# Walking both halves of a gated linear recurrence through their levels together, in a one-core encoder block

## The chip, the cores and the metric

The kernel runs on one core of one Trainium2 chip. A core has five engines that run their own instruction queues: TensorE (PE, matrix products), VectorE (DVE), ScalarE (ACT), GpSimd (POOL) and SyncE (SP, which only starts transfers here). Transfers between the chip's main memory and the core's on-chip memory go through DMA queues. The metric is the device time of one execution in microseconds; lower is better. Three executions of the kernel before took 2413.86, 2413.97 and 2415.13 us (median 2413.97 us).

## What is computed

The reference is one layer of a streaming-encoder block on 256 tokens of width 2048, all in 32-bit floats:

```python
x = x + 0.5 * swiglu(rms_norm(x, ffn1_norm[l]), ffn1_w_up[l], ffn1_w_down[l])
h = rms_norm(x, mix_norm[l])
proj = h @ w_in[l]
q_a, f_a, i_a, g_a, x_b, gate_b, gates = jnp.split(proj, splits, axis=-1)
o_a = hgrn2_chunked(q_a..., f_a..., i_a..., lb)        # gated linear recurrence, 8 heads
y_a = rms_norm(o_a, hgrn_norm[l]) * silu(g_a)
y_b = rglru_branch(x_b, gate_b, ...)                   # conv(4), then an associative scan
merged = g[:, :, 0] * (y_a @ w_branch_a[l]) + g[:, :, 1] * (y_b @ w_branch_b[l])
x = x + merged @ w_out[l]
x = x + cross_attention(rms_norm(x, xattn_norm[l]), rms_norm(mem, mem_norm[l]), ...)
x = x + 0.5 * swiglu(rms_norm(x, ffn2_norm[l]), ffn2_w_up[l], ffn2_w_down[l])
return rms_norm(x, final_norm)
```

The part that the change touches most is the gated linear recurrence. For each of 8 heads the state is S_t = diag(f_t) S_{t-1} + (1 - f_t) outer v_t and the output o_t = S_t^T q_t; it is not computed token by token.

## The kernel before, in words

**Weights.** Nearly all the time goes to products of the 256 tokens with weight tiles of 128 x 2048 numbers. Each weight comes in by one transfer into a tile `raw`; ACT copies it, rounded, into `h`, and DVE subtracts to get the rest, `l`. PE multiplies with both, which keeps the precision of 32-bit floats. `raw`, `h`, `l` and a few others share a ring of nine large buffers called `big`. Between the two SwiGLU parts there are 160 such weights: 48 for the input projection (`win`, `wv`), 32 gate weights (`wg`), then the branch, output, query, key and output weights of the rest. On PE a weight of the input projection is a row of 16 matmuls with `h` and one of 16 with `l` (`acc<-ops,h`, `acc<-ops,l`); a value or gate weight has 16 and 8 (`acc<-h,ops`, `acc<-l,ops`).

**The recurrence.** `hgrn(hf)` (from line 1264) is a Python generator that writes down the work for half the heads, four of them: `q`, `f` and `k` for 128 features x 4 heads x 256 tokens. It goes through seven levels (1, 2, 4, ... 64 tokens). At each level PE makes small products of `k` with `q` (`acc<-silu,k`: blocks of 32 partitions up to level 32, then 64 and 128), DVE masks them into the tile `S`, and DVE multiplies one half of `q` and one of `k` by the running products `tots`. Behind the levels come the outputs (`acc<-S,v`, two banks for two heads), their squares on ACT (`osq`), a sum over features on PE (`acc<-osq,ones`), a root on ACT (`ostd`), and on DVE two `RECIPROCAL`s and four products into `ya`. This is done twice, for two heads each. Each `yield` is a point at which the main loop goes on with another weight. `lru(hf)` (line 1366), the other recurrence, has the same form.

The main loop walks a list of units; behind each unit it takes steps of the first generator in the list `side`:

```python
    units += [lambda hf=hf: side.append(hgrn(hf)) or True]      # behind each half's 16 weights

    for u in units:
        if not u():
            pump(2)
```

So the first half's levels are written between the second half's input weights, and the second half's levels behind those.

**Sums made ahead.** The second SwiGLU part needs for 56 of its up-projection tiles four differences of quarter tiles each. They are made during the 160 weights in the middle: `make_sums` loads a tile (`made<-wu`, started by POOL), DVE does four subtractions of 128 x 512 (`made<-made`), and POOL starts the store (`kept<-made`). `make_ahead` spreads the 56 over a number of weights that `between` and a constant set.

**What sets the order.** Nothing runs in the order in which it was written. Every operation is recorded (`Flow.record`), and a planner (`arrange`) gives each a price and a due time, and plays the engines forward: each takes the ready operation with the earliest due time, as far as a free buffer is there. The sequence that comes out is the program; each engine then runs its part of it strictly in that order. Buffers are given out in the same pass, the eight banks in which PE accumulates (`psum`, tag `acc`) too. All instructions of the profile carry line 478, where the sequence is issued, so one goes by the names of the tiles.

The pools for the middle part are opened in one line. `scores` holds the tile `S` of a half, and `tmp2` the tiles `junk` and `ostd`:

```python
    middle.enter_context(scope(tmp=8, tmp2=2, scores=1, extra=2, feature=3))
```

## Time and profile before

| | |
|---|---|
| median of three executions | 2413.97 us |
| the profiled execution: its time, its span | 2415.09 us, 2413.3 us |
| PE busy in the span | 2401.9 us (100%) |
| DVE busy | 2088.1 us (87%) |
| ACT busy | 1441.9 us (60%) |
| granted TensorE clock | 0.999 |
| first and last load for a sum made ahead | 849.3 and 1690.8 us |
| first and last small product of the recurrence | 884.1 and 1103.9 us |

A row of a timeline gives the start in us from the start of the span, the length in us, the engine, the operation, output<-inputs, the size, and in how many instructions; what stands in brackets is the idle time before it and what ended it. PE shows a 32-bit product as two passes, so 32 products of `k` with `q` read as x64. PE's instructions overlap: the step from the start of one to the start of the next tells what each costs, not its length. The same holds on DVE to a lesser degree.

### The profile page before, as it was taken

How to read it: one execution, taken by the hardware profiler on the slowest of the kernel's cores; microseconds unless marked ns; L12 is line 12 of the kernel's file. 1: busy time of each engine (PE TensorE's matmuls, PEld its weight loads, DVE VectorE, ACT ScalarE, POOL GpSimd, SP SyncE). 2: the span in 40 equal slices, each digit the busy share in tenths (PEclk: the TensorE clock that was granted, in tenths of full speed). 3: DMA queues.
4: the chain of work that ended last, by engine and by line, in shares of the span. 5: the costliest groups of instructions: out<-in, count | busy, mean ns of one | idle time of the engine just before them, and what ended most of it. 6: DMA issues, size and time to landing. Idle time of an engine off the chain costs nothing. (4 is left out here: it accounts for less than half of the span.)

```text
span 2413.3 us, 31006 instructions
## 1 busy us (share of the span) xinstructions
PE 2401.9 (100%) x12105; PEld 2005.3 (83%) x12105; DVE 2088.1 (87%) x2270; ACT 1441.9 (60%) x1432; POOL 88.3 (4%) x149
## 2 busy tenths in 40 slices
PE   9999999999999999999999999999999999999998
PEld 8888788888888888888888888888888788888887
DVE  7899999999996578888787878887799999999995
ACT  8765666766665444445853455555676666666663
POOL 0000000000000000000000000000000000000000
PEclk9999999999999999999999999999999999999999
DMA  9675877787884578798898898887798677777773
GB/s 367 242 277 181 262 261 250 257 259 255 254 258 177 190 293 317 273 347 331 332 336 334 322 367 341 333 311 274 271 378 325 244 261 262 261 262 261 262 272 116
DMA packets 101235, 674.37 MB, mean 279 GB/s; under 512 B 11232, under 2 KB 12000, under 8 KB 27232
## 3 DMA queue, kind: packets, MB, share of 16 engines
q1 hardware_dynamic: 79776, 523.40, 58.0%
q0 software_dynamic: 20592, 147.86, 19.0%
q8 instruction: 95, 1.56, 0.3%
q10 hardware_dynamic: 720, 1.13, 0.1%
q14 instruction: 52, 0.43, 0.0%
HBM read 581.12 MB, written 62.91 MB: 267 GB/s over the span
## 5 line engine op out<-in xcount | busy, mean ns | idle before, releaser
L478 DVE TENSOR_TENSOR l<-raw,h 128x2048 fp32r<-128x2048 f32 (+2 forms) x425 | 859.2, 2025 | 170.2 <-ACT h L478 78.2
L478 ACT ACTIVATE h<-raw 128x2048 fp32r<-128x2048 f32 (+2 forms) x425 | 721.8, 1704 | 380.6 <-PE acc L478 166.4
L478 PE MATMUL acc<-h,xh 128*128 128x512 f32 x1237 | 473.6, 391 | 1.0 <-DVE x L478 0.5
L478 PE MATMUL acc<-h,xl 128*128 128x512 f32 x1237 | 472.0, 389 | 0.0
L478 ACT ACTIVATE h<-td 128x1024 fp32r<-128x1024 f32 (+1 forms) x262 | 322.8, 1241 | 228.2 <-DVE td L478 204.2
L478 DVE TENSOR_TENSOR tl<-td,h 128x1024 fp32r<-128x1024 f32 (+1 forms) x262 | 374.8, 1445 | 5.1 <-PE acc L478 2.1
L478 PE MATMUL acc<-h,hidop 128*128 128x512 f32 x1408 | 355.8, 390 | 0.0
L478 PE MATMUL acc<-h,ops 128*128 128x512 f32 x1408 | 336.8, 391 | 0.0
L478 PEld LDWEIGHTS acc<-h,hidop 128*128 128x128 f32 x1408 | 262.8, 188 | 53.9
L478 PEld LDWEIGHTS acc<-h,ops 128*128 128x128 f32 x1408 | 262.7, 188 | 53.9
L478 PE MATMUL acc<-ops,h 128*128 128x512 f32 x1152 | 282.0, 393 | 0.2 <-DVE ops L478 0.2
L478 PEld LDWEIGHTS acc<-h,xh 128*128 128x128 f32 x1237 | 231.8, 188 | 53.8 <-ACT h L478 3.1
L478 PEld LDWEIGHTS acc<-h,xl 128*128 128x128 f32 x1237 | 232.3, 188 | 47.7
L478 PEld LDWEIGHTS acc<-ops,h 128*128 128x128 f32 x1152 | 211.4, 188 | 42.3 <-DVE ops L478 0.6
L478 PE MATMUL acc<-l,hidop 128*128 128x512 f32 x704 | 193.5, 389 | 0.4 <-DVE l L478 0.4
L478 PE MATMUL acc<-tl,xh 128*128 128x512 f32 x636 | 175.4, 392 | 0.8 <-DVE tl L478 0.7
L478 PE MATMUL acc<-l,ops 128*128 128x512 f32 x704 | 174.3, 389 | 0.0
L478 PE MATMUL acc<-l,xh 128*128 128x512 f32 x601 | 167.8, 390 | 0.0
L478 DVE TENSOR_TENSOR made<-made 128x512 f32<-128x512 f32 x224 | 152.1, 687 | 8.6 <-DMA made<-wu 5.2
L478 PEld LDWEIGHTS acc<-ops,l 128*128 128x128 f32 x1152 | 150.5, 191 | 6.4
L478 PEld LDWEIGHTS acc<-l,hidop 128*128 128x128 f32 x704 | 132.1, 188 | 28.2 <-DVE l L478 0.8
L478 PEld LDWEIGHTS acc<-l,ops 128*128 128x128 f32 x704 | 132.1, 188 | 27.4
(172 smaller groups left out, 2132.4 us busy)
## 6 DMA issues: line engine op xcount, KB each, us to landing
raw<-wu SPq DMA_DIRECT2D x109, 1024.0 KB, 6.2
raw<-wd SPq DMA_DIRECT2D x72, 1024.0 KB, 6.8
made<-wu POOLq DMA_DIRECT2D x56, 1024.0 KB, 6.7
kept<-made POOLq DMA_DIRECT2D x56, 1024.0 KB, 6.8
td<-kept SPq DMA_DIRECT2D x56, 1024.0 KB, 7.2
raw<-wu SPq DMA_DIRECT2D x56, 768.0 KB, 6.0
raw<-win SPq DMA_DIRECT2D x40, 1024.0 KB, 4.9
raw<-wg SPq DMA_DIRECT2D x32, 1024.0 KB, 7.1
```

Source lines behind the costliest of these rows:

```text
L478: getattr(op.queue.real, method)(*map(real, args), **{k: real(v) for k, v in kw.items()})
```

## The change

The change takes three steps.

The two halves of the recurrence are no longer started one behind the other. A new helper, `both`, takes one step of each in turn, so that level by level first half 0 and then half 1 is written, and the pair is put into `side` once, behind the second half's 16 weights. For this there are two tiles `S`. The pool `tmp2` goes from two buffers to one.

The sums made ahead begin four weights sooner: `between` starts 8 weights ahead of the end of the first SwiGLU part's list and no longer 4. The number of weights over which they are spread stays 140 (160 less 20 before, 164 less 24 now), so they end four weights sooner too.

```diff
-    between = between - 4, len(plan) - between
+    between = between - 8, len(plan) - between + 4
     plan_ffn("ffn2", wu2, wd2)
...
     def make_ahead(i):
-        n, pieces = len(MADE), between[1] - 20
+        n, pieces = len(MADE), between[1] - 24
         if 0 <= i < pieces:
             for j in range(i * n // pieces, (i + 1) * n // pieces):
                 makers.append((i + 2, make_sums(*MADE[j])))
...
-    middle.enter_context(scope(tmp=8, tmp2=2, scores=1, extra=2, feature=3))
+    middle.enter_context(scope(tmp=8, tmp2=1, scores=2, extra=2, feature=3))
...
+    def both(parts):
+        while parts:
+            for p in list(parts):
+                try:
+                    more = next(p)
+                except StopIteration:
+                    parts.remove(p)
+            if parts:
+                yield more
+
     units = []
     for hf in range(2):
...
-        units += [lambda hf=hf: side.append(hgrn(hf)) or True]
+    units += [lambda: side.append(both([hgrn(hf) for hf in range(2)])) or True]
```

**On PE, the small products.** Before, each half has its own runs of them between the weights. Here is the end of the first half's levels, where the outputs begin (`silu` is the tile of `q`; `v_6510` and `v_6516` are the values of the two halves of the tokens):

```order
L478 MATMUL acc<-silu,k 128x128 x4
L478 MATMUL acc<-ops,h 128x512 x16
L478 MATMUL acc<-ops,l 128x256 x16
L478 MATMUL acc<-S,v_6510 128x256
L478 MATMUL acc<-S,v_6516 128x128
L478 MATMUL acc<-S,v_6510 128x256
L478 MATMUL acc<-S,v_6516 128x128
L478 MATMUL acc<-ops,h 128x512 x16
L478 MATMUL acc<-ops,l 128x256 x16
L478 MATMUL acc<-osq,ones 128x256 x2
```

The same place in the changed kernel, where it lies among the gate weights:

```order
L478 MATMUL acc<-silu,k 128x128 x8
L478 MATMUL acc<-h,ops 128x512 x16
L478 MATMUL acc<-l,ops 128x512 x8
L478 MATMUL acc<-S,v_6520 128x256
L478 MATMUL acc<-S,v_6526 128x128
...
L478 MATMUL acc<-osq,ones 128x256 x2
L478 MATMUL acc<-h,ops 128x512 x16
L478 MATMUL acc<-l,ops 128x512 x8
L478 MATMUL acc<-osq,ones 128x256 x2
```

Eight rows with `S` stand there in one run and not four (the rows left out repeat the two above them three times), and a sum over squares follows at once, in the same run. In all, the runs of 32-bit products (those with `silu,k`, `S,v`, `osq`, `xc,lw`, the transposes and a few others) are 76 on PE before and 65 after; all eleven that go lie in the recurrence, which has 24 before (18 of levels, 6 of outputs and sums) and 13 after (9 and 4).

**On DVE, behind the levels.** Before, the second half's first `RECIPROCAL`s stand between the `l` of gate weights, counted from 0, number 8 to 11:

```order
L478 TENSOR_TENSOR made<-made 128x512 x3
L478 RECIPROCAL ostd<-ostd 128x256
L478 TENSOR_TENSOR l<-raw,h 128x2048
L478 TENSOR_TENSOR made<-made 128x512
L478 TENSOR_TENSOR l<-raw,h 128x2048
L478 TENSOR_TENSOR ya<-acc,ostd 128x256
L478 RECIPROCAL ostd<-ostd 128x256
L478 SCALAR_TENSOR_TENSOR ya<-ya,vt,silu 128x256
L478 TENSOR_TENSOR l<-raw,h 128x2048
```

In the changed kernel four of the eight stand behind the `l` of gate weight 4, with no other `l` until gate weight 5's, which comes 21 instructions later:

```order
L478 TENSOR_TENSOR l<-raw,h 128x2048
L478 TENSOR_TENSOR made<-made 128x512 x3
L478 RECIPROCAL ostd<-ostd 128x256
L478 TENSOR_TENSOR made<-made 128x512
L478 TENSOR_TENSOR ya<-acc,ostd 128x256
L478 RECIPROCAL ostd<-ostd 128x256
L478 SCALAR_TENSOR_TENSOR ya<-ya,vt,silu 128x256
L478 TENSOR_TENSOR ya<-acc,ostd 128x256
L478 SCALAR_TENSOR_TENSOR ya<-ya,vt,silu 128x256
L478 SCALAR_TENSOR_TENSOR xc<-plain,vt,xc 128x255 x2
L478 RECIPROCAL ostd<-ostd 128x256
```

**On DVE, the first sums made ahead**, one piece of the difference (+ is the changed kernel), among the second group of input weights:

```order
-L478 TENSOR_TENSOR l<-raw,h 128x2048
 L478 TENSOR_TENSOR silu<-silu,sum 128x256
-L478 TENSOR_TENSOR sum<-acc,lo 128x256
-L478 TENSOR_TENSOR sum<-sum,rstd 128x256
-L478 TENSOR_TENSOR l<-raw,h 128x2048
+L478 TENSOR_TENSOR l<-raw,h 128x2048
+L478 TENSOR_TENSOR made<-made 128x512 x3
+L478 TENSOR_TENSOR sum<-acc,lo 128x256
+L478 TENSOR_TENSOR made<-made 128x512
```

Four subtractions `made` stand there now, of which the kernel before has none so early. On POOL's queue the zeroing of `S` is now two `MEMSET`s in a row, behind 12 loads of tiles for sums; before it was one behind 3 and one behind 12.

## The prediction

> **What bounds the kernel now.** I read the busy times first, then PE's waits, then PE's timeline through the recurrence, and last DVE's lead over PE there.

> ```profile
> PE 2401.9 (100%) x12105; PEld 2005.3 (83%) x12105; DVE 2088.1 (87%) x2270; ACT 1441.9 (60%) x1432; POOL 88.3 (4%) x149
> ```
> ```profile
> PE warm L478 <- DVE ones L478: 1.1, 1, 1.1
> PE acc L478 <- DVE tl L478: 0.7, 3, 0.3
> PE acc L478 <- DVE x L478: 0.5, 1, 0.5
> PE acc L478 <- DVE l L478: 0.4, 1, 0.4
> PE acc L478 <- DVE ev L478: 0.3, 1, 0.3
> PE acc L478 <- DVE ops L478: 0.2, 1, 0.2
> PE acc L478 <- ACT h L478: 0.2, 1, 0.2
> ```
> ```profile
> 840.00:980.00 140.00, 140.00 (x1153) 121.05 (x1152) 105.36 (x140) 62.79 (x69) 10.17 (x18) 1.00 0.81 294
> 980.00:1130.00 150.00, 150.00 (x1184) 128.97 (x1183) 123.36 (x159) 67.37 (x69) 12.30 (x22) 1.00 0.86 320
> 1900.00:2300.00 400.00, 399.81 (x1792) 330.40 (x1791) 392.11 (x343) 244.32 (x192) 0.00 (x0) 1.00 0.71 261
> ```

> PE is busy all through; its waits (who for whom: total, times, longest) add to 3.4 us, of which 1.1 stands at the start. In the stages (length, then busy time of PE, weight loads, DVE, ACT, POOL, then clock and DMA) the clock is full. So the kernel is as long as PE's instructions, and a change can gain only by making PE's own work shorter, plus at most 2.3 us of waits. It loses whatever makes PE wait. DVE is the engine to watch: 105 of 140 us where the first half of the recurrence runs, 123 of 150 in the second, 392 of 400 late in the second SwiGLU.

> **The small products.** The change adds and removes no matmul. It turns 24 runs of 32-bit products into 13. What does a run cost beside its products?

> ```profile
> 888.53 2.07 PE L478 MATMUL acc<-ops,l 128*128 128x256 f32 x16
> 890.54 0.74 PE L478 MATMUL acc<-silu,k 128*32 128x16 f32 x64
> 891.20 3.92 PE L478 MATMUL acc<-ops,h 128*128 128x512 f32 x16
> 894.96 2.08 PE L478 MATMUL acc<-ops,l 128*128 128x256 f32 x16
> 896.87 3.82 PE L478 MATMUL acc<-ops,h 128*128 128x512 f32 x16
> 900.53 2.07 PE L478 MATMUL acc<-ops,l 128*128 128x256 f32 x16
> ...
> 974.36 1.05 PE L478 MATMUL acc<-silu,k 128*128 128x128 f32 x8
> 975.17 3.92 PE L478 MATMUL acc<-ops,h 128*128 128x512 f32 x16
> 978.93 2.08 PE L478 MATMUL acc<-ops,l 128*128 128x256 f32 x16
> 980.84 1.47 PE L478 MATMUL acc<-S,v 128*128 128x256 f32 x8
> 982.07 3.23 PE L478 MATMUL acc<-ops,h 128*128 128x512 f32 x13
> ```
> ```profile
> L478 PE MATMUL acc<-silu,k x880: 182/183/276, 884.1 to 1103.9; 128*32 128x16 f32 x128, 128*32 128x32 f32 x40, 128*64 128x64 f32 x6, 128*128 128x128 f32 x2
> ```

> Without a run between, `l` to the next `h` is 896.87 - 894.96 = 1.91 us and `h` to `l` 900.53 - 896.87 = 3.66. With one they are 891.20 - 888.53 = 2.67 and 894.96 - 891.20 = 3.76. The run costs 0.76 + 0.10 = 0.86 us. Its 64 passes start over 0.74 - 0.18 us (a pass lasts 183 ns, the middle number of the last row), so 8.9 ns apart: 0.57 us for 64. The other 0.29 us is paid per run, for going into small blocks and out again. Two runs in one pay it once, seven times (levels 1 to 32 and the diagonal): 7 x 0.29 = 2.03 us. For full-width passes only the slower first matmuls behind the run are sure, 978.93 - 975.17 - 3.66 = 0.10 us. I take 0.10 for the last level, 0.20 for 64-wide blocks, and 2 x 0.15 for the two runs of outputs and sums that go. Sum: 2.6 us less, between 11 x 0.10 = 1.1 and 11 x 0.29 = 3.2.

> [...]

> **What else is on PE's path: DVE's work, now bunched.** Both halves' level work now falls between the same input weights:

> ```profile
> L478 DVE TENSOR_TENSOR made<-made 128x512 f32<-128x512 f32 x224 | 152.1, 687 | 8.6 <-DMA made<-wu 5.2
> L478 DVE RECIPROCAL ostd<-ostd 128x256 f32<-128x256 f32 x8 | 13.9, 1744 | 1.1 <-ACT ostd L478 1.1
> ```

> Through the levels the total hardly moves. From the `l` of input weight 35 (of 48, from 0) to that of gate weight 4 the changed order has 136 DVE instructions, the one before 119; with each at its length less the 0.08 us by which DVE's instructions overlap (shown below) that is 89 us against 87, since before the first half's last products and more of `made` stood there. PE has 17 weights of at least 5.44 us there, 92 us, and the longer runs. The order leaves two weights, 11 us, from level to level, and a level's four products of 0.69 us (as long as `made`, which has the same 512 elements) are 2.8. I cost the levels at nothing; if that cover goes, each costs PE what DVE is late.

> It is tighter behind the levels. From the `l` of gate weight 4 to that of gate weight 13 the changed order gives DVE 84 instructions: 9 `l` of 2.20 us, 8 reciprocals of 1.66, 20 subtractions `made` of 0.60, 21 of `xc` of 0.40, 16 of `ya` of 0.34, 4 gates of 0.66 and `lru`'s four long ones, 66 us (the overlap: below, 1132.51 - 1132.18 = 0.33 us where the length is 0.42). PE needs for nine weights 9 x 5.44 = 49 us (1144.80 - 1139.36, below), and for a run of sums and one of `lru` in between about 4: 53 us. DVE loses 13 us of its lead. How much lead is there? The first `l` below is used at 1095.89, the second at 1114.48:

> ```profile
> 1083.16 2.28 DVE L478 TENSOR_TENSOR l<-raw,h 128x2048 fp32r<-128x2048 f32 x1
> 1098.33 2.28 DVE L478 TENSOR_TENSOR l<-raw,h 128x2048 fp32r<-128x2048 f32 x1
> 1116.27 1.41 DVE L478 SCALAR_TENSOR_TENSOR gate<-acc,rtok,bgate 128x512 f32<-128x512 f32 x2 [1.93 <-PE acc L478]
> 1132.18 0.42 DVE L478 TENSOR_TENSOR ya<-acc,ostd 128x256 f32<-128x256 f32 x1
> 1132.51 1.74 DVE L478 RECIPROCAL ostd<-ostd 128x256 f32<-128x256 f32 x1
> 1140.84 2.28 DVE L478 TENSOR_TENSOR l<-raw,h 128x2048 fp32r<-128x2048 f32 x1
> ```
> ```profile
> 1095.89 1.98 PE L478 MATMUL acc<-l,ops 128*128 128x512 f32 x8
> 1114.48 1.98 PE L478 MATMUL acc<-l,ops 128*128 128x512 f32 x8
> 1139.36 1.98 PE L478 MATMUL acc<-l,ops 128*128 128x512 f32 x8
> 1144.80 1.98 PE L478 MATMUL acc<-l,ops 128*128 128x512 f32 x8
> ```

> That is 10.5 and 13.9 us; and the last `l`, used at 1144.80, shows 1.7 left where the second half's reciprocals stand now. With 13.9 the lead comes down to about 1 and PE hardly waits; with 10.5 PE waits 2.5 us, and 4.4 if DVE also waits once for PE as it does before the gates here (1.93 us). I take 1.0 us, nearest the 13.9 (a lead taken just ahead of the gate weights, as it would be here); ends 0 and 4.4.

> **The sums made ahead.** The same 224 subtractions (152 us of DVE) and 112 transfers begin and end four weights, 22 us, earlier, at a time when DVE was at 75% or less. Nothing waits for them before the second SwiGLU. Zero, with DVE's free time as cover; from -0.5 us to +0.5 us from DVE's different load at the start of the second SwiGLU, whose waits for `tl` are part of the 0.7 above. The second tile `S` frees the second half's zeroing on POOL from waiting; zero, no one waits there. The one buffer for `ostd` makes ACT's next root wait for two reciprocals, and ACT's later `h` behind it; with leads of 10 us zero, else part of the 4.4.

> **The sum.** 2415.09 (the profiled execution) - 2.6 + 1.0 = 2413.5 us. The median of the three runs, 2413.97, is 1.1 below the profiled one; the same sum from it is 2412.4 us, which I predict. 0.2% (4.8 us) is about what a measurement of this kernel can tell from no change, so this is "no change", slightly on the fast side.

> **The rivals.**

> *The output banks (slower).* PE accumulates in eight banks. With both halves at their outputs, four hold results of the first two heads of each half, two a gate weight's, and the sums take more, so PE's next `S` run must wait until DVE has read a bank into `ya`. From the start of the first `S` run: two times 1.23 us of `S` (982.07 - 980.84), the last squares on ACT (0.38 each), table load and root, then reciprocal, `made` and `ya`:

> ```profile
> 1110.35 0.38 ACT L478 ACTIVATE osq<-acc 128x256 f32<-128x256 f32 x1 [4.53 <-PE acc L478]
> 1129.78 1.28 ACT L478 ACT_TABLE_LOAD   x1
> 1131.08 0.69 ACT L478 ACTIVATE ostd<-acc,few 128x512 f32<-128x512 f32 x1
> ```

> 2.46 + 0.9 + 1.28 + 0.69 + 1.74 + 0.69 + 0.42 = 8.2 us. PE comes to that run after 2.46 + 0.9 of sums + 5.44 + 0.9 = 9.7. The margin is 1.5 us. Three subtractions `made` stand on DVE ahead of that reciprocal, and they need a load:

> ```profile
> DMA to landing us min/median/max: 4.1/6.7/12.7
> DVE made L478 <- DMA made<-wu: 5.2, 4, 2.2
> ```

> A load as late as the longest (6.0 us over the median) costs PE 6.0 - 1.5 = 4.5 us: 2412.4 + 4.5 = 2416.9, slower than before from 1.6 + 1.5 = 3.1 us of lateness on. Against it: DVE waited for such loads four times in 224, 2.2 us at the most. [...]

> *The waits go too (faster).* DVE's load in the second SwiGLU falls so that the 2.3 us of waits behind the start vanish, none comes at the gates, and the saving is at its upper end: 2413.97 - 3.2 - 2.3 = 2408.5. For it: DVE ends the sums 22 us earlier. Against it: the largest waits lie in stages that the change does not touch.

> [...]

> *It does not do what it says.* Switching is paid per level and half anyway, inside the merged run: -0.4 for the rest, + 1.0: 2414.6.

> **How the numbers follow.** Forecast 0.56; banks 0.22, half of it with more than one late load and over 2418.8; waits go too 0.12, nearly all beyond 2409.1; passes at 4 ns 0.05; nothing merged 0.05. Faster by over 0.2%: 0.11. Slower: 0.11. Within: 0.78. The range leaves out the lower half of the fast case and the upper half of the banks': 2408.9 to 2418.0.

> **What would show it.** Runs `silu,k` of x128, about 0.18 + 127 x 0.0089 = 1.3 us long, in 9 places, and 13 runs in all; PE busy about 2399 us; the gap between `l` and its use down to about 1 us at gate weight 13; waits of PE for `l` or `ya` of 0 to 4 us between 1090 and 1160; the first load for a sum near 827 us, the last near 1669. It is wrong if PE waits at the `S` runs, if a level finds DVE not ready, or if the second SwiGLU, where DVE has 2% left, begins with DVE behind.

## The result, and the profile after

The changed kernel takes 2420.77 us, the median of seven runs; the kernel before, in seven runs on the same chip, 2413.97. The ratio is 1.0030, with a 95% interval from 1.0021 to 1.0040: slower by 0.3%, 6.8 us, where I had forecast 2412.4 and no change. The runs spread more than before: 2418.85 to 2425.35 us, against 2413.42 to 2415.93. The profiled execution is the fastest of them, 2418.85 us with a span of 2417.0 (before: 2413.3), so its trace holds 3.7 of the 6.8 us.

The busy times, and PE's waits (who for whom: total, times, longest) of the changed kernel:

```profile
PE 2398.5 (99%) x12105; PEld 2004.8 (83%) x12105; DVE 2088.9 (86%) x2270; ACT 1440.2 (60%) x1430; POOL 88.2 (4%) x149
```
```profile
PE acc L478 <- issue: 5.1, 2, 2.8
PE acc L478 <- DVE tl L478: 1.5, 3, 1.0
PE acc L478 <- DVE ops L478: 1.5, 2, 1.3
PE warm L478 <- DVE ones L478: 1.1, 1, 1.1
PE acc L478 <- ACT h L478: 0.7, 2, 0.5
...
```

PE's own work shrank by 3.4 us, to about the 2399 that I had forecast. Its waits grew from 3.4 to 10.4 us, and half of that is a kind that the profile before does not have: "issue", time in which the engine waited for nothing that the profile shows. The chain of waits from 970 to 1015 us has both of them, and PE's timeline shows what stands around each:

```profile
969.93 10.69 PE acc L478 x218
980.62 2.31 issue
982.93 24.26 PE acc L478 x325
1007.20 2.78 issue
1009.98 5.12 PE acc L478 x27
```
```profile
976.20 2.07 PE L478 MATMUL acc<-ops,l 128*128 128x256 f32 x16
978.20 1.30 PE L478 MATMUL acc<-silu,k 128*32 128x16 f32 x128
979.42 1.20 PE L478 MATMUL acc<-ops,h 128*128 128x512 f32 x4
982.93 2.93 PE L478 MATMUL acc<-ops,h 128*128 128x512 f32 x12 [2.31 <-issue]
...
1005.87 1.33 PE L478 MATMUL acc<-silu,k 128*32 128x16 f32 x128
1009.98 3.36 PE L478 MATMUL acc<-ops,h 128*128 128x512 f32 x14 [2.78 <-issue]
```

Each stands behind a merged run of x128. The first is inside one input weight: four of its 16 products run, then PE stands still, though the same tile `h` feeds the other twelve. No data is missing there. So what was?

**The instructions themselves.** The page's list of DMA queues has a line that I had passed over:

```profile
q8 instruction: 95, 1.56, 0.2%
```

Packets, MB, share: 95 packets of 16 KB during the kernel. PE's instructions in the trace (12,105 products, 12,105 weight loads, 149 others) are 24,359: 256.4 to a packet, or 95.15 blocks of 256. In experiment 12 PE has 2,560 more than before and the queue ten packets more, which is 256 to a packet. So I take it that PE's program comes in through the DMA engines while it runs, 256 instructions at a time. Counted from 0 in the order of their starts, the instruction at which PE stopped is 9665 the first time and 10433 the second: both are number 193 of a block of 256 (37 x 256 + 193 and 40 x 256 + 193). Here and below 193 is good to one instruction, since a weight load and the product ahead of it overlap and their order is read from their starts. The packets that end the waits begin at 980.67 and 1007.64, last 0.97 and 0.94 us, and PE goes on 1.3 and 1.4 us after each has landed.

A merged run is 128 products and 128 weight loads: a whole block, gone in 1.3 us. Theory A is that PE stops because it uses up its instructions faster than the next block comes. A block lasts PE 22 to 29 us where only big products stand; where a merged run falls in it, much less. What starts a fetch the trace doesn't show. Its beginning follows, by 1.4 to 10.4 us over all fetches of the kernels before and after, the moment at which PE is 320 instructions short of the one that will need it; so I reckon with 320 instructions of cover, an estimate from these two traces. If a run of 256 lies wholly in them, the other 64 are 32 big products, and the cover is 7.0 us of PE's time. In the changed kernel four fetches have about 7 us of it; in the kernel before, whose runs are 128 instructions, the least is 10.4. Of the four, the two that came late began 7.2 us after that moment, the other two 4.2 and 3.7. The closest that a block came to being late before was 4.0 us ahead of its use.

The rest of the span, by PE's place in the work (after less before): 1.5 us ahead by input weight 16, in code that did not change; 3.0 lost from there to gate weight 25; 1.7 at the queries (`ops`); 0.8 at `tl`; 0.3 regained between.

### The profile page after: what moved, and what is told of

It is laid out like the page before. It is cut to its first block, busy times and chain, and to the rows that moved or that the text cites. A ratio compares the mean times of both kernels' runs of the same rounds, so it can differ in the third digit from the quotient of the medians.

```text
span 2417.0 us, 31003 instructions
## 1 busy us (share of the span) xinstructions
PE 2398.5 (99%) x12105; PEld 2004.8 (83%) x12105; DVE 2088.9 (86%) x2270; ACT 1440.2 (60%) x1430; POOL 88.2 (4%) x149
## 4 chain that ended last, share of the span: by engine, by line
PE 95%; DVE 2%; DMA 2%; issue 1%; ACT 1%; SPq 0%; ACTq 0%; DVEq 0%; POOLq 0%
PE acc L478 95%; DMA raw<-wvm 1%; DMA l<-own 1%; DVE tl L478 0%; DVE td L478 0%; DVE l L478 0%; DVE ev L478 0%; DMA own<-wd 0%; ACT h L478 0%; DVE x L478 0%; SPq L478 0%; ACT ops L478 0%; ACT x L478 0%; DVE hidop L478 0%; ACT ev L478 0%
## 5 line engine op out<-in xcount | busy, mean ns | idle before, releaser
L478 DVE TENSOR_TENSOR l<-raw,h 128x2048 fp32r<-128x2048 f32 (+2 forms) x425 | 859.4, 2026 | 183.7 <-ACT h L478 90.2
L478 ACT ACTIVATE h<-raw 128x2048 fp32r<-128x2048 f32 (+2 forms) x425 | 721.4, 1703 | 355.9 <-PE acc L478 166.7
L478 PE MATMUL acc<-h,xh 128*128 128x512 f32 x1237 | 473.3, 391 | 1.2 <-ACT h L478 0.7
L478 PE MATMUL acc<-h,xl 128*128 128x512 f32 x1237 | 471.6, 389 | 0.0
L478 ACT ACTIVATE h<-td 128x1024 fp32r<-128x1024 f32 (+1 forms) x262 | 322.8, 1241 | 229.6 <-DVE td L478 198.3
L478 DVE TENSOR_TENSOR tl<-td,h 128x1024 fp32r<-128x1024 f32 (+1 forms) x262 | 374.5, 1445 | 4.9 <-PE acc L478 2.3
L478 PE MATMUL acc<-h,hidop 128*128 128x512 f32 x1408 | 355.5, 390 | 0.0
L478 PE MATMUL acc<-h,ops 128*128 128x512 f32 x1408 | 336.7, 391 | 0.0
L478 PEld LDWEIGHTS acc<-h,ops 128*128 128x128 f32 x1408 | 263.1, 188 | 53.9
L478 PEld LDWEIGHTS acc<-h,hidop 128*128 128x128 f32 x1408 | 262.9, 188 | 53.7
L478 PE MATMUL acc<-ops,h 128*128 128x512 f32 x1152 | 281.7, 393 | 6.6 <-issue 5.1
L478 PEld LDWEIGHTS acc<-h,xh 128*128 128x128 f32 x1237 | 231.7, 188 | 53.4 <-ACT h L478 3.5
L478 PEld LDWEIGHTS acc<-h,xl 128*128 128x128 f32 x1237 | 232.2, 188 | 47.8
L478 PEld LDWEIGHTS acc<-ops,h 128*128 128x128 f32 x1152 | 211.6, 188 | 49.3 <-issue 5.8
L478 PE MATMUL acc<-l,hidop 128*128 128x512 f32 x704 | 193.6, 389 | 0.0
L478 PE MATMUL acc<-tl,xh 128*128 128x512 f32 x636 | 174.6, 391 | 1.6 <-DVE tl L478 1.5
L478 PE MATMUL acc<-l,ops 128*128 128x512 f32 x704 | 173.9, 389 | 0.0
L478 PE MATMUL acc<-l,xh 128*128 128x512 f32 x601 | 167.5, 390 | 0.0
L478 DVE TENSOR_TENSOR made<-made 128x512 f32<-128x512 f32 x224 | 152.7, 687 | 12.4 <-DMA made<-wu 8.9
L478 PEld LDWEIGHTS acc<-ops,l 128*128 128x128 f32 x1152 | 150.7, 191 | 6.5
L478 PEld LDWEIGHTS acc<-l,hidop 128*128 128x128 f32 x704 | 132.1, 188 | 27.6 <-DVE l L478 0.2
L478 PEld LDWEIGHTS acc<-l,ops 128*128 128x128 f32 x704 | 132.2, 188 | 27.5
```

Source lines behind the costliest of these rows:

```text
L478: getattr(op.queue.real, method)(*map(real, args), **{k: real(v) for k, v in kw.items()})
```

## The experiments

Theory B, the first rival, was that the transfers of the sums made ahead, now 22 us earlier, starve PE. Theory C was that it is the two halves at one level: their tiles, banks, DVE and ACT. Comparisons are with runs of the kernel before in the same set (2414.96 us median in the first, 2414.59 in the second, 2415.22 in the third).

**1. The sums' shift alone**

```diff
-    between = between - 4, len(plan) - between
+    between = between - 8, len(plan) - between + 4
...
-        n, pieces = len(MADE), between[1] - 20
+        n, pieces = len(MADE), between[1] - 24
```

> Only the sums made ahead move four weights; the two halves of the recurrence stay one behind the other. Theory A (PE ran out of instructions behind the merged runs of 128 small products: the two waits of PE marked issue, 5.1 us, in the changed kernel): no wait marked issue here, runs stay at 64 products; what is left of the change is the waits of PE for ops near 1448 (1.5 us) and for tl near 1913 (0.8 more than before), so 2 to 3 us over the kernel before, about 2416.5. Theory B (the loads and stores of the sums, 22 us earlier, crowd the DMA engines and that alone starves PE): the waits marked issue are here too, 3 to 5 us, near 980 and 1010, and the time is 2418 to 2421.

2417.81 us, ratio 1.0014 (1.0005 to 1.0023): 2.9 us slower. No wait marked issue, and no block closer than 4.6 us. PE's waits, for `ops` above all, add to 5.0 against 3.4 us:

```profile
PE acc L478 <- DVE ops L478: 1.2, 3, 0.6
...
```

So theory B falls, and a term that I had at zero is 2.9 us. The waits hold 1.6 of it; where the rest went is not shown. The place in the second SwiGLU that I had named (`tl`) is not where it went: 0.7 us, as before.

**2. The levels alone** (`both`, and the tiles for `S` and `ostd`; `between` as before)

> Only the two halves go through their levels together (with the two tiles S and one for ostd); the sums made ahead stay where they were. Theory A: PE busy falls to about 2398.5 as in the changed kernel, the waits marked issue stand behind one to three of the merged runs of 128, 2 to 6 us in all, the waits for ops near 1448 and tl near 1913 are as small as before (0.2 and 0.7): 2413 to 2417. Theory B: no wait marked issue, 2.6 us of saving is left whole: 2411 to 2412.

2423.44 us, ratio 1.0035 (1.0022 to 1.0047), above the 2413 to 2417 of theory A. The waits marked issue are there without the sums' shift, at the same two instructions 9665 and 10433. And something more happens behind them: PE's clock falls. The waits begin at 982.29 and 1010.56 us and last 2.35 and 2.58. PE's waits, and windows behind each of the two (length, PE busy, granted clock, DMA share, GB/s):

```profile
PE acc L478 <- issue: 4.9, 2, 2.6
PE acc L478 <- ACT h L478: 3.1, 5, 1.4
```
```profile
985.30:988.70 3.40, 3.40 (x10) 0.51 0.67 265
988.80:992.00 3.20, 3.20 (x23) 1.00 0.82 276
1012.60:1016.00 3.40, 2.86 (x7) 0.51 0.99 383
```

For 3.4 us PE runs at half speed, so each of the two waits, of 2.35 and 2.58 us, costs 1.7 more. Small products, 1.3 us of them, stand ahead of these waits (more on those at 6), but they are not needed: the clock also fell behind a wait of 1.88 us for `x` in the first SwiGLU part of experiment 5, and behind one of 2.27 us for `h` in experiment 8, both among large products alone (the same columns, first of 5, then of 8):

```profile
434.70:438.00 3.30, 3.30 (x10) 0.50 1.02 271
```
```profile
1456.20:1459.50 3.30, 3.30 (x8) 0.50 1.01 410
```

The length of the wait alone doesn't decide it: the profiled execution of the changed kernel shows no such window although its waits are 2.31 and 2.78 us: the granted clock is 1.00 from 985 to 990 us and from 1010 to 1015. Three of its seven runs have a granted clock of 0.997 against its 0.999, and they are the three over 2424 us; that the clock fell at the same places there is inferred, not seen.

Also, the waits for `h` add to 3.1 us, 2.4 of it behind the levels, at gate weights 12 to 17 (0.2, 0.8 and 1.4 between 1150 and 1185 us). Experiment 10 takes that up. And the waits for `tl` are 1.5 us, where I had expected the 0.7 of the kernel before: with 0.7 in experiment 1, they come with the levels and not with the sums' shift.

**3. The instruction stream shifted**

```diff
     for _ in range(16):
         pe.matmul(warm[:, :P], ones, ones, start=True, stop=True)
+    for _ in range(18):
+        pe.matmul(warm[:, :8], ones, ones[:, :8], start=True, stop=True)
```

> The changed kernel with 18 more tiny products (8 columns) behind the 16 that warm PE at the start, where PE waits for its first weight: all later work is unchanged, but PE's instruction stream is 36 instructions longer ahead of the levels. Theory A: in the changed kernel both waits marked issue begin at the same place of a 16 KB block of instructions (instruction 193 of 256, counted from the trace), where a merged run of 256 instructions lies whole in the last 320 ahead of it; 36 more instructions move the runs so that 26 fewer of them lie there at the second and fourth merged run, some 2 us more time. Waits marked issue fall from 5.1 to between 0 and 1.5 us (the first merged run, then wholly inside, may now wait up to 1 us), time 2414.5 to 2417. Any theory by data, buffers, engines or DMA load alone: nothing changes, 5 us of waits marked issue at the same two products, 2419 to 2421.

2419.87 us (2417.73 to 2421.65), 1.0020 (1.0011 to 1.0029). A miss in part: an fp32 product is two passes (68 rows of `warm` at the start against 32), so 72 instructions were added and not 36, and they cost 4 us at the start: the first weight's products begin at 10.51 us, against 6.54 in the changed kernel, and the first 16 of them last 5.51 us against 4.32. With 72, again four fetches have 7.5 us of cover or less. But the waits went where the count says, not where they had been: one of 1.3 us in the page, inside other products than before, once more at instruction 193 of a block, number 39 x 256 + 193:

```profile
1000.20 1.83 PE L478 MATMUL acc<-ops,l 128*128 128x256 f32 x14
1003.32 0.40 PE L478 MATMUL acc<-ops,l 128*128 128x256 f32 x2 [1.29 <-issue]
```

Nothing of the data, the buffers or the order had changed. This speaks for A, and against every theory by data.

**4. No sums around the merged runs**

```diff
-            for j in range(i * n // pieces, (i + 1) * n // pieces):
+            active = lambda i: max(0, min(i, 34)) + max(0, i - 54)
+            for j in range(active(i) * n // (pieces - 20), active(i + 1) * n // (pieces - 20)):
```

> The changed kernel, but no sum is made ahead for 20 of the 140 weights, those around the merged runs (the other 120 take 0.93 sums each in place of 0.80). Theory A in its full form (the fetch of the next 16 KB of instructions stands in the DMA queues behind loads and stores of 1 MB): the fetch begins some 3 us sooner and the waits marked issue fall to 0 to 1 us; the denser sums elsewhere cost 0 to 3 us: 2414 to 2418. If only the count of instructions matters and not the DMA load: 5 us of waits marked issue stay, 2419 to 2422.

2431.34 us, 1.0073 (1.0060 to 1.0085). It did not make its own condition: started sums were emptied late, and the DMA share from 970 to 981 us was 1.01, against 0.91 from 970 to 983 in the changed kernel. One wait marked issue stayed (2.6 us, instruction 9665), the other went; the moved sums cost 8.6 us of waits for `h` elsewhere. It says nothing on the DMA's part.

**5. The kernel before, each small product issued twice**

```diff
                     s = slice(g * P + b, g * P + b + 32)
-                    pe.matmul(acc[b:b + 32, i * n:(i + 1) * n], kv[:, h, s], pick(qv[:, h, s]), start=True, stop=True)
+                    for _ in range(2):
+                        pe.matmul(acc[b:b + 32, i * n:(i + 1) * n], kv[:, h, s], pick(qv[:, h, s]), start=True, stop=True)
```

> The kernel before (halves one behind the other, sums where they were), but each product of the 32-wide runs is issued twice, the second over the first: runs as long as the merged ones (256 instructions), of one half only, with two weights from run to run. Theory A: waits marked issue appear here too, each beginning at instruction 193 of 256 of a 16 KB block, 1 to 3 us each, 4 to 14 us in all over the twelve runs; PE's busy time grows by 12 runs x 0.57 = 6.8 us, the time by 11 to 24 us (more where the clock falls behind a wait). Theory C (what starves PE comes from the two halves being at the same level: their tiles, banks, DVE, ACT): no wait marked issue, 6.8 us more and no more.

2428.81 us, 1.0059 (1.0041 to 1.0077), two runs. Three waits marked issue, 2.9 us in all, all at instruction 193 of a block, with one half at a time and no buffer changed; one falls inside a run of small products:

```profile
1028.80 0.34 PE L478 MATMUL acc<-silu,k 128*32 128x16 f32 x17
1029.93 1.26 PE L478 MATMUL acc<-silu,k 128*32 128x16 f32 x111 [0.79 <-issue]
```

Theory C falls. The total is below my 4 to 14 us: counted as above, six fetches had 7.5 us of cover or less, and three of them came in time, so little cover makes a wait possible and not certain.

**6. Bursts of dummy products far from the levels**

```diff
+    def burst(accs, n):
+        for _ in range(n):
+            pe.matmul(accs[0][:32, :8], ones[:, :32], ones[:, :8], start=True, stop=True)
```
(ahead of the gates' groups 4 to 7 with n = 32, 64, 96, 128; ahead of the output's groups 0 to 3 with 128, 96, 64, 32)

> The kernel before, with tiny dummy products (32 rows of the array's columns, 8 columns, overwritten by the product behind them) in eight places far from the levels: ahead of the gates' groups 4 to 7, bursts of 128, 256, 384 and 512 instructions, and ahead of the output's groups 0 to 3 of 512, 384, 256 and 128. Theory A: no wait marked issue behind 128; 0 to 3 us behind 256, as the burst lies to the 16 KB blocks; 2 to 8 us behind each of 384 and 512, beginning at instruction 193 of a block; so some 10 to 30 us of it in all, where no half of a recurrence is. If the waits come from the recurrence's data: none anywhere.

2483.8 us, and only one wait marked issue, 1.9 us. The expectation was wrong on the speed: products that all write the same group of 32 columns ran at 36 ns a pass (128 passes in 4.66 us), four times the 8.9 of the levels, whose products go round four groups. At that pace PE outran its fetches once, in a burst of 384. The run showed something else: behind 128 such passes the clock was at half for 6.8 us with no wait at all (0.85 granted from 1190 to 1196 us, 0.64 from 1196 to 1203), behind 64 passes (2.19 us) it was not. At this pace small products did to the clock what a wait did.

**7. The stream shifted by 168** (as 3, with 42 products of `ones[:, :32]` and `ones[:, :8]` into `warm[:32, :8]`: 84 passes, 168 instructions)

> The changed kernel with 168 more instructions of PE at the very start (84 passes of 32 x 8, some 0.75 us by 8.9 ns each), so that of the merged runs only one lies wholly in the 320 instructions between the start of a fetch and the instruction that needs it, in place of four. Theory A: waits marked issue fall from 5.1 to 0 to 2.6 us, and the spread of the runs with it; 2416 to 2419.5. By data, buffers or engines: 5 us as before, 2420 to 2423.

2414.74 us (2413.89 to 2416.86), ratio 1.0001 (0.9992 to 1.0010), below the 2416 to 2419.5 that I had expected. With 168 instructions more, the kernel is 0.3% faster than the changed kernel: no wait marked issue, one fetch with 7.0 us of cover and the next with 8.7, and the spread is gone with the waits.

**8. The pause of the sums ten weights earlier** (24 and 44 for the 34 and 54 of 4)

> As the pause of the sums before, but the 20 weights without a sum begin ten weights earlier, since the kernel empties its started sums late and the pause before left the transfers at 950 to 985 as dense as they were. If the fetch of instructions waits behind the transfers of the sums, the first merged runs (970 to 990) now find a DMA share of 0.5 to 0.7 and no wait marked issue there, and one may come at the last runs; if the DMA load does not matter, one wait of 2 to 3 us stays near 981. The time is not the point here: the sums that are moved cost waits elsewhere, 2422 to 2434.

2423.97 us. No wait marked issue, but the block needed at instruction 9665 came with nothing to spare, and the DMA share was again high (1.00 from 955 to 970 us, 0.89 from 970 to 981). What makes a fetch begin 1.4 us after its turn at one time and 7.2 at another stays open: my two attempts to thin out the transfers there did not do so.

**9. The changed kernel, stream shifted by 168 at less cost**

```diff
+    for i in range(42):
+        pe.matmul(warm[i % 4 * 32:][:32, :8], ones[:, :32], ones[:, :8], start=True, stop=True)
```

> The changed kernel with 168 more instructions of PE at the start, as in the shift by 168 before, but the dummy products go round the four column groups, as those of the levels do (8.9 ns a pass there), instead of standing in one: 84 passes are 0.75 us and not the 2.8 us that the start took longer. Theory A: no or one short wait marked issue (0 to 2 us), what remains is the 2.2 us saved at the merged runs against 2 us of new waits for ops and tl: 2413 to 2415.5. By data, buffers or engines: 2420.

2413.37 us (2412.29 to 2414.2), ratio 0.9992 (0.9983 to 1.0001): against 1.0030 without the 168 instructions, and the fastest of all, though not surely faster than the kernel before. No wait marked issue:

```profile
PE acc L478 <- DVE ops L478: 1.9, 2, 1.7
PE acc L478 <- DVE tl L478: 1.5, 3, 1.0
PE warm L478 <- DVE ones L478: 1.1, 1, 1.1
PE acc L478 <- ACT h L478: 0.7, 2, 0.5
PE acc L478 <- DVE ev L478: 0.3, 1, 0.3
```

Here the merged runs can be priced clean. PE's rows at the start of input weight 16 and of gate weight 25, of the kernel before and then of this one:

```profile
872.86 1.32 PE L478 MATMUL acc<-ops,h 128*128 128x512 f32 x5
...
1218.82 3.56 PE L478 MATMUL acc<-h,ops 128*128 128x512 f32 x15
```
```profile
870.86 1.32 PE L478 MATMUL acc<-ops,h 128*128 128x512 f32 x5
...
1214.53 3.79 PE L478 MATMUL acc<-h,ops 128*128 128x512 f32 x16
```

345.96 and 343.67 us: the levels together save 2.3 us. PE waits for nothing in this stretch in either trace. The same stretch takes 343.71 us in experiment 7, and 345.96 and 346.06 in experiments 1 and 11, where the levels stay apart.

**10. The levels alone, stream shifted by 168** (2 with the lines of 9)

> Only the levels together (sums where they were), with the same 168 instructions at the start. Theory A: the 4.9 us of waits marked issue and the two half-clock windows behind them (about 1.7 us each) go to 0 to 2.5 us; the waits for h, l and x behind the levels (4 us) stay: 2414.5 to 2418, against 2423.4 without the 168. By data or engines: 2422 to 2424.

2417.41 us, 1.0010 (1.0001 to 1.0019), 6.0 us under 2 by 168 dummy instructions. No wait marked issue, and a granted clock of 0.999 in all eleven runs (in 2 it was 0.998 in four of five). What is left stands behind the levels, where DVE and ACT are late with the weights; PE's waits, and its rows there:

```profile
PE acc L478 <- ACT h L478: 4.2, 5, 1.4
...
PE acc L478 <- DVE l L478: 0.8, 2, 0.7
```
```profile
1142.18 3.94 PE L478 MATMUL acc<-h,ops 128*128 128x512 f32 x16 [1.26 <-ACT h L478]
1146.29 2.11 PE L478 MATMUL acc<-l,ops 128*128 128x512 f32 x8 [0.16 <-DVE l L478]
...
1154.64 3.94 PE L478 MATMUL acc<-h,ops 128*128 128x512 f32 x16 [0.80 <-ACT h L478]
...
1159.24 2.11 PE L478 MATMUL acc<-l,ops 128*128 128x512 f32 x8 [0.66 <-DVE l L478]
...
1177.08 3.26 PE L478 MATMUL acc<-h,ops 128*128 128x512 f32 x13 [1.37 <-ACT h L478]
```

Against 9 it is 4.0 us slower. So the sums' shift, which costs 2.9 us by itself, is worth 4.0 with the levels together.

**11. Control: the kernel before with the lines of 9**

> Control: the kernel before with the same 168 instructions at the start. Theory A: there was no wait marked issue to take away, so only the start's up to 0.8 us: 2414 to 2416. If the dummy products help by themselves (a warmer PE, another start of the transfers), it is faster than before by as much as the changed kernel gained, 2408 to 2410.

2414.59 us, 0.9998 (0.9989 to 1.0007). The dummy instructions help only where merged runs are.

**12. The bursts of 6, round the four column groups** (`accs[0][i % 4 * 32:][:32, :8]`)

> The bursts of dummy products far from the levels once more, now round the four column groups, as the first time they all stood in one group and ran at 36 ns a pass. Theory A: 8.9 ns a pass, so 0.6, 1.1, 1.7 and 2.3 us for 128, 256, 384 and 512 instructions; no wait marked issue behind 128, 0 to 3 us behind 256, 2 to 8 us at 384 and 512, each beginning at instruction 193 of a block. If the waits come from the recurrence's data: none.

One run, 2455.61 us. Now the bursts run at 9 ns a pass (128 passes in 1.26 us). PE's rows at the bursts of 128, 256, 384 and 512 instructions and at the second 512, and the instruction queue's:

```profile
1166.35 0.72 PE L478 MATMUL acc<-ones 128*32 128x8 f32 x64
1189.00 1.26 PE L478 MATMUL acc<-ones 128*32 128x8 f32 x128
1215.65 1.49 PE L478 MATMUL acc<-ones 128*32 128x8 f32 x156
1220.43 0.49 PE L478 MATMUL acc<-ones 128*32 128x8 f32 x36 [3.29 <-issue]
1244.43 2.29 PE L478 MATMUL acc<-ones 128*32 128x8 f32 x252
1251.49 0.28 PE L478 MATMUL acc<-ones 128*32 128x8 f32 x4 [4.77 <-issue]
...
1365.03 2.33 PE L478 MATMUL acc<-ones 128*32 128x8 f32 x256
1373.10 5.79 PE L478 MATMUL acc<-h,ops 128*128 128x512 f32 x14 [5.07 <-issue]
```
```profile
q8 instruction: 105, 1.72, 0.3%
```

Nothing behind 128 and 256, 3.3 to 5.1 us at each of the four longer ones, 18.2 in all, each at instruction 193 of a block, and the clock at half for 3.4 or 6.8 us behind them (0.57 granted from 1221 to 1225 us; 0.74 from 1246 to 1251 and 0.58 from 1251 to 1256). The last line is of the list of DMA queues: 2,560 instructions more than before are ten blocks, and the queue has ten packets more. No recurrence is near.

## Why the prediction was wrong

**The step that failed** is the first of the sum, "The change adds and removes no matmul. It turns 24 runs of 32-bit products into 13." I asked what a run costs and what a merged run saves, and never what a run of 256 instructions in 1.3 us asks of whatever supplies PE with instructions. The supply was in the page (queue 8), and my list of what could make PE wait held data, banks and engines only. No rival had it. In the profile it is 5.1 us, twice the saving, and in experiment 2 two stretches of 3.4 us at half clock, 3.4 us more; experiments 3, 5, 7, 9, 10 and 12 tie it to the count of instructions. By the ratios, 1.0030 without the 168 instructions of experiment 9 and 0.9992 with them, it is some 9 us in all. My account of the runs was also off in a smaller way: six of the nine merged runs have 128 passes (the others 64, 32 and 16), where I had written nine.

**The saving** was right: 2.6 us forecast, 2.3 measured in experiment 9, and PE's busy time of 2398.5 us in the changed kernel where I had said about 2399. That experiment 9 as a whole lies 1.9 us under the kernel before, where I had forecast 1.6, is luck: its trace is 2.0 us ahead by input weight 16, in code that did not change but for the 168 instructions, and then loses 2.2 us at the queries, to which I had given nothing.

**The wait behind the levels** was right in place and close in size. I forecast a lead of about 1 us at gate weight 13 and a wait of 1.0 us, with 4.4 as the far end. In the changed kernel the first `l` of DVE's row below ends 2.28 us after its start, at 1154.1, and PE takes it at 1155.20: a lead of 1.1 us, and no wait.

```profile
1151.80 4.46 DVE L478 TENSOR_TENSOR l<-raw,h 128x2048 fp32r<-128x2048 f32 x2
```
```profile
1155.20 1.98 PE L478 MATMUL acc<-l,ops 128*128 128x512 f32 x8
```

With the sums where they were the lead is gone: 4.2 us of waits at gate weights 12 to 17 in experiment 10. That this is near my far end is chance, since I had taken the lead to be the same whether the sums move or not.

**The sums made ahead** were mis-sized. I said zero, at most 0.5 us either way; alone they cost 2.9 us (experiment 1), and with the levels they bring 4.0 back (10 against 9). "Nothing waits for them before the second SwiGLU" was true of the sums and not of the instructions that DVE ran in their place: at the queries of the changed kernel DVE, whose order had changed, stood waiting ahead of an `l`, and the four `ops` that PE needed came behind it:

```profile
1445.66 2.29 DVE L478 TENSOR_TENSOR l<-raw,h 128x2048 fp32r<-128x2048 f32 x1 [3.39 <-ACT ops L478]
1447.87 1.65 DVE L478 SCALAR_TENSOR_TENSOR ops<-acc,vt,ops 128x256 fp32r<-128x256 f32 x4
```
```profile
1448.40 1.74 PE L478 MATMUL acc<-ops,h 128*128 128x512 f32 x5 [1.27 <-DVE ops L478]
```

PE has no wait there in experiments 2 and 10, with the sums where they were, and one of 1.73 us in experiment 9. That the shift changed DVE's order is seen; why the planner made that order is not.

**The rivals.** The output banks did not come: no wait of PE at the runs of `S`, no late load there. The waits did not go. The chances have 0.05 for passes at 4 ns, and no run shows such a step: small products ran at 8.9 ns a pass in the kernel before, at 9 in experiment 12 and at 36 in experiment 6, and the saving was 2.3 us. Of the signs that I named for being wrong none fits the main loss: PE was kept waiting at the levels, though not by DVE. The third comes nearest to the smaller one, 0.8 us more for `tl` in the second SwiGLU.

## What to carry to other kernels

Count the instructions that an engine must be given in the densest stretch, not only their time: here PE stood still for 2.31 and 2.78 us behind 256 in 1.3 us, and the fetch of a block of 256 more began 1.4 to 10.4 us after PE was 320 instructions short of needing it. A wait marked issue that begins at the same number of a fixed block, whatever the product, was the sign here (number 193 of 256); shift the stream (here by 72 and by 168 instructions) and see whether the wait moves or goes. Merging runs of tiny products may be worth less than keeping them apart with big products between: here it saved 2.3 us and brought 5.1 us of waits.
